# Attention with values as weights in two column halves, logits' products on 128 rows, and layer 0's u splits placed by the scheduler

## The chip, the cores and the metric

One core of one Trainium2 chip runs the whole program in one launch. The metric is the device time of one execution in microseconds (us). TensorE (PE) multiplies, PEld is its weight load, VectorE (DVE) and ScalarE (ACT) do elementwise work, GpSimd (POOL) gathers, SyncE (SP) issues most of the DMAs. Each engine works through its own queue in order.

## What is computed

A decoder step of two layers, d = 1024, for 512 prompt tokens and 8 sample tokens. Layer 0 mixes tokens with a gated delta rule (4 heads, chunks of 64) and a gated linear recurrence (RG-LRU); layer 1 with sliding-window attention (16 query heads, 4 key heads of 64, window 128, a learned sink logit per head). Behind each mixer stands a PEER block: 8 heads pick 16 of 16384 experts, and an expert e adds g_e * v_e * gelu(u_e . x).

```python
x = LN(alpha*x + mixer(x)); x = LN(alpha*x + peer(x))          # each layer
...
logits = (q @ k.T) * 64**-0.5 + bias                           # mixer of layer 1, per head
m = max(logits.max(-1), sink); p = exp(logits - m)             # masked to the window
o = (p / (p.sum(-1) + exp(sink - m))) @ v
...
h = gelu(x @ u_tab.T); y = (gates * h) @ v_tab                 # peer, over the experts picked
```

## The kernel before, in words

A tile scheduler orders each engine's queue: it goes through the program text with a model of each operation's time, and where several instructions are ready, the one that stands earlier in the text goes first. The order on the chip is fixed when the program is built.

Float32 products of projections are made of three float16 products: a number is split into a high half (`split`, first line: ACT copies and rounds, L72) and a low half (second line: DVE takes source times scale less the high half, L79 or L81), and `mm3` (L86 to L88) multiplies high by high, high by low and low by high.

**The u splits.** PEER's dense part multiplies by the table `in_uT` of each layer, block by block. For the first blocks the split halves are made ahead, while a mixer runs, and kept in a DRAM buffer `PW`: `presplit` loads a half block `pst` (128 x 512, 256 KB, issued by SP, L106), splits it to `ppr` (ACT L72, DVE L81) and stores it (SP, L111). `peer` reads `PW` back as `wpr` much later. Layer 0 has 16 blocks or 32 halves, layer 1 has 12 blocks or 24 halves. Before the change `presplit` is a generator. For layer 0 `pstep()` advances it by one half at places chosen in the text of `mixer_ab`: in `new_states`, seven times in the second `inverse`, twice behind each chunk group `rec(n)`, behind each column half of the output projection `mix_out`, with a loop at the end for what is left. `pstep` also ties the half behind the last instruction that DVE and ACT have had in the text (`issue_after`). Each half is one ACT and one DVE instruction of 128 x 512, and `pst` and `ppr` have two buffers each. For layer 1 it is a plain loop behind `mixer_c`, in two pieces of 128 x 256 per half, and the scheduler places it.

**Layer 0's mixer** runs: projections and RG-LRU; `pairs_` (decays `dT`, L1033, and products of the chunks' keys) for chunk groups 0 and 1; `inverse((0, 1))`, with tiles `ia` to `ie` that ACT copies out of PSUM; `zproj` (the z projection, `zth` on ACT, L1169); `pairs_` 2 and 3; `new_states`, which loads the samples' states `S0` (`in_state_gdn`, SP, L1174) and stores the new ones; `inverse((2, 3))`; `rec` (the recurrence over four groups); `mix_out` with `w_out_ab` (residual `mixx`, layer norm L173 to L181, transposes L190, `xh`/`xl`). PEER's queries follow, whose first DVE work is the top-k (L253).

**Layer 1's attention**, `block(n)` for four blocks of 128 queries: for each key-head pair a and head pair q (16 rounds in all), the logits are the sum of a product with the keys' high half `kh` (128 rows, L1444) and one with the low half `kl` (the 64 rows of one half, L1445) for two key heads j and two query heads r; DVE adds the bias and takes the maximum (L1448); ACT takes the exponential and the row sums (L1459); DVE makes the reciprocal of the denominator (L1463); PE transposes the probabilities (L1470), ACT copies them to `pT`; PE multiplies with `pT` as weights (128 columns) and the values `vt` (64 columns) as moving data (L1475, float32, which the trace shows as two records each); DVE multiplies the result by the reciprocal into `ot` (L1477). When a block has its four rounds, PE transposes `ot` in eight pieces (L1484) and `split` makes `mh`, `ml` of it, the moving data of the output projection.

Of the kernel before, what the change touches and what calls it, by code (L numbers as in the profile page):

```python
# [20 lines left out]
PB, PC = 2, 2  # L21
# [44 lines left out]
class Kern:  # L66
# [32 lines left out]
    def presplit(self, pool, layer, n, parts=2):  # L99

        nc, A = self.nc, self.A
        for b in range(n):
            for hf in range(2):
                c = slice(4 * hf, 4 * hf + 4)
                st = pool.tile([P, 4, P], F32, name="pst")
                nc.sync.dma_start(st, A["uT"][layer, b][:, c])  # L106
                o = pool.tile([P, 2, 4, P], F16, name="ppr")
                for q in range(0, 4, 4 // parts):
                    x = slice(q, q + 4 // parts)
                    self.split(o[:, 0, x], o[:, 1, x], st[:, x], SCW)  # L110
                nc.sync.dma_start(self.PW[layer, b, :, :, c], o)  # L111
                yield

    def behind(self, ins):

        ctx = ExitStack()
        for i in ins:
            ctx.enter_context(self.tc.issue_after(i))
        return ctx

    def last_on(self, *engines):

        ins = self.nc.cur_bb.bb.instructions
        return [next(i for i in reversed(ins) if i.engine == e.engine) for e in engines]
# [71 lines left out]
    def mix_out(self, psum, pool, mh, ml, woh, wol, layer, tags, bias=None, bufs=2, step=lambda: None):  # L196
# [12 lines left out]
        for t, t1 in zip(order, order[1:] + (None,)):  # L209
            n = P if t < 4 else NS  # L210
            if t1 is not None:
                load(t1)
            c = slice(t * P, t * P + n)
            x = xs[t][:n]
            if bias is not None:
                nc.vector.tensor_add(x, x, bias[:n])
            if t == 4:

                ps = psum.tile([P, 512], F32, name="pmix", tag=tags[0], bufs=bufs)
                for kb in (4, 5, 6, 7, 0, 1, 2, 3):  # L220
                    for i, (a, b) in enumerate(((mh, woh), (mh, wol), (ml, woh))):
                        for g in range(4):
                            nc.tensor.matmul(ps[32 * g:32 * g + NS, 0:256], a[:, kb, c],
                                             b[kb][:, g * 256:g * 256 + 256], start=kb == 4 and i == 0,
                                             stop=kb == 3 and i == 2)
                s4 = pool.tile([P, 256], F32, name="mixs4")
                s1 = self.wst.tile([P, D], F32, name="wst")[:NS]
                for g in range(4):
                    self.copy(s4[32 * g:32 * g + NS], ps[32 * g:32 * g + NS, 0:256], 1.0 / (SCW * ALPHA))
                    nc.scalar.dma_start(s1[:, g * 256:g * 256 + 256], s4[32 * g:32 * g + NS])  # L230
                nc.vector.tensor_add(x, x, s1)
            for h in range(2 if t < 4 else 0):
# [6 lines left out]
                if t1 is not None:  # L239
                    step()  # L240
# [451 lines left out]
    def mixer_ab(self, ctx):  # L692
# [354 lines left out]
        def inverse(C4, late=False):  # L1047
# [9 lines left out]
            late and pstep()  # L1057
# [11 lines left out]
            late and pstep()  # L1069
# [8 lines left out]
            late and pstep()  # L1078
# [3 lines left out]
            late and pstep()  # L1082
# [3 lines left out]
            for wd in (16, 32):  # L1086
# [3 lines left out]
                late and pstep()  # L1090
# [6 lines left out]
                late and pstep()  # L1097
# [144 lines left out]
        def new_states(ks, vn, egs):  # L1242
# [5 lines left out]
            for q in range(NS):  # L1248
# [5 lines left out]
                if q % 2:  # L1254
                    pstep()
# [19 lines left out]
        inverse((2, 3), True)  # L1275
        ictx.close()
        for n in range(4):
            rec(n)
            pstep()
            pstep()  # L1280
        nc.sync.dma_start(A["o_pgdn"], st)
        with scope("about"):
# [6 lines left out]
            self.mix_out(psum, cur[0], mh, ml, woh, wol, 0, ("g0", "g1", "p", "a"), step=pstep)  # L1289
            for _ in split:  # L1290
                pass
# [41 lines left out]
    def mixer_c(self, ctx):  # L1333
# [38 lines left out]
        kl = w([P, 2, NP], "kl", F16)  # L1372
# [10 lines left out]
        while porder:  # L1383
# [24 lines left out]
            if b in (8, 9):  # L1408
                for j in range(2):
                    o, x = half[j], half[1 - j]  # L1410
                    self.split(kh[o, b - 8, j], kl[o, b - 8], kv[o, b - 8, 0:NP], SQK)
# [17 lines left out]
        def block(n):  # L1429
# [3 lines left out]
            ot = ap_.tile([P, 2, 2, 2, 2, 64], F32, name="ot", bufs=2)  # L1433
            for a in range(2):
                for q in range(2):
# [28 lines left out]
                    po = ps1("o")  # L1464
                    for r in range(2):
                        pt = ps1("t").rearrange("p (j b k) -> p j b k", j=2, b=2)
                        pT = ap_.tile([P, 2, 2, P], F32, name="pT", bufs=4)
# [12 lines left out]
            of = ot.rearrange("p a q r s d -> p (a q r s d)")  # L1480
            for c in range(2):
                pt = ps1("t")
                for k in range(4):
                    T.transpose(pt[:, k * P:k * P + P], of[:, (c * 4 + k) * P:(c * 4 + k + 1) * P], self.ident)  # L1484
                self.split(mh[:, c * 4:c * 4 + 4, tq], ml[:, c * 4:c * 4 + 4, tq],
                           pt.rearrange("p (k t) -> p k t", k=4))
# [74 lines left out]
    def run(self):  # L1561
        nc, tc, A = self.nc, self.tc, self.A
        with ExitStack() as ctx:
# [28 lines left out]
            with ExitStack() as c:  # L1592
                self.mixer_ab(c)
            self.xd = [xd0, xd1]
            self.peer(0)
            with ExitStack() as c:
                pre = self.mixer_c(c)
                for _ in self.presplit(pre, 1, self.NPRE[1]):
                    pass
# [142 lines left out]
```

## Time and profile before

| what | us |
|---|---|
| median of 3 runs | 3039.98 (3039.46 to 3040.66) |
| the profiled execution | 3032.15 |
| its span in the trace | 3030.5 |
| layer 0's mixer | 0 to about 386 |
| layer 0's PEER | to about 1581 |
| layer 1's mixer | to about 1829 |
| layer 1's PEER | to 3030 |

A window's row gives, for each engine, busy time and, in brackets, instructions; PEclk is the granted TensorE clock as a share of full speed. The profiled execution is 7.8 us under the median of the runs.

### The profile page before, as it was taken

The numbers are of one execution on the slowest core, as the hardware profiler recorded it, in microseconds if no ns is written. First come the engines' busy times: TensorE is split into PE (matmuls) and PEld (weight loads), VectorE is DVE, ScalarE is ACT, GpSimd is POOL, SyncE is SP. The second block draws the span as 40 slices with busy tenths as digits, with TensorE's granted clock in tenths as the row PEclk, the third lists the DMA queues.
The fourth block names the chain that finished last, engine by engine and source line by source line (L and its number), as shares of the span: only waits on it lengthen the run. The fifth ranks groups of instructions, "written<-read, shape, count | busy, mean of one in ns | idle before, by whom it ended". The sixth has DMA issues, their size and how long they took to land.

```text
span 3030.5 us, 49817 instructions
## 1 busy us (share of the span) xinstructions
PE 2882.0 (95%) x18342; PEld 1754.9 (58%) x18342; DVE 2557.2 (84%) x5783; ACT 1315.6 (43%) x2131; POOL 838.5 (28%) x661
## 2 busy tenths in 40 slices
PE   8999899899999999999998999989999999999998
PEld 7787586466655555544447568645665555554443
DVE  6755899999878888899986558989987898898998
ACT  4733442356743333333336623335665333343332
POOL 2300101400034555445520000131002445444552
PEclk9998999999999999999999799999999999999999
DMA  4225645965699999999968212586658999999996
GB/s 136 71 81 187 215 126 202 302 225 206 215 375 374 371 359 363 357 352 371 351 243 252 92 63 92 173 303 214 215 202 319 390 363 357 359 360 355 363 356 234
DMA packets 332105, 798.79 MB, mean 264 GB/s; under 512 B 28611, under 2 KB 165259, under 8 KB 328020
## 3 DMA queue, kind: packets, MB, share of 16 engines
q1 hardware_dynamic: 241004, 442.78, 43.2%
q0 software_dynamic: 78336, 285.25, 25.4%
q10 hardware_dynamic: 12520, 67.58, 6.0%
q8 instruction: 143, 2.34, 0.3%
q14 instruction: 102, 0.84, 0.1%
HBM read 700.96 MB, written 93.17 MB: 262 GB/s over the span
## 4 chain that ended last, share of the span: by engine, by line
PE 63%; DVE 15%; DMA 10%; ACT 6%; issue 5%; POOL 1%; SPq 0%; ACTq 0%; DVEq 0%; POOLq 0%
PE yps L623 29%; PE pu L88 6%; PE pu L86 6%; PE pu L87 6%; DMA GD<-stage 3%; ACT stage L72 2%; DMA pst<-in_uT 2%; DVE wl L81 2%; DMA row<-in_u_rows,elist 2%; DVE row L380 1%; PE psg L1009 1%; ACT wh L72 1%; POOL row L373 1%; PE pq L87 1%; PE pq L86 1%
## 5 line engine op out<-in xcount | busy, mean ns | idle before, releaser
L623 PE MATMUL yps<-vv,vw 128*128 128x512 f16 x4536 | 1011.4, 379 | 10.8 <-ACT vv L72 9.0
L623 PEld LDWEIGHTS <-vw 128*128 128x128 f16 x4608 | 450.2, 98 | 542.7 <-issue 16.3
L88 PE MATMUL pu<-xh,wl 128*128 128x384 f16 x1824 | 598.9, 329 | 33.1 <-DVE wl L81 32.7
L373 POOL DMA_INDIRECT row<-in_v_rows,elist x272 | 378.4, 1391 | 886.8 <-ACT stage L72 452.7
L86 PE MATMUL pu<-xh,wh 128*128 128x384 f16 x1824 | 599.4, 329 | 16.1 <-ACT act L349 12.1
L87 PE MATMUL pu<-xl,wh 128*128 128x384 f16 x1824 | 599.6, 329 | 0.0
L373 POOL DMA_INDIRECT row<-in_u_rows,elist x272 | 390.6, 1436 | 673.6 <-DVE best L253 252.2
L72 ACT ACTIVATE wh<-wst 128x1024 f16<-128x1024 f32 x296 | 312.4, 1056 | 554.7 <-PE pu L87 351.2
L81 DVE SCALAR_TENSOR_TENSOR wl<-wst,wh 128x1024 f16<-128x1024 f32 x296 | 361.5, 1222 | 147.2 <-ACT wh L72 136.3
L88 PEld LDWEIGHTS <-wl 128*128 128x128 f16 x2912 | 287.1, 99 | 187.1 <-DVE wl L81 47.0
L86 PEld LDWEIGHTS <-wh 128*128 128x128 f16 x2912 | 289.7, 100 | 160.1 <-ACT wh L72 25.5
L87 PEld LDWEIGHTS <-wh 128*128 128x128 f16 x2912 | 287.2, 99 | 151.8 <-issue 17.8
L72 ACT ACTIVATE vv<-row 128x1024 f16<-128x1024 f32 x252 | 263.2, 1048 | 237.4 <-PE yps L623 183.0
L81 DVE SCALAR_TENSOR_TENSOR vv<-row,vv 128x1024 f16<-128x1024 f32 x252 | 307.7, 1222 | 52.1 <-ACT vv L72 50.6
L561 DVE SCALAR_TENSOR_TENSOR yac<-row,wgt,yac 128x1024 f32<-128x1024 f32 x268 | 343.5, 1282 | 2.8 <-DMA row<-in_v_rows,elist 1.1
L380 DVE CUSTOM_DVE_ANT_0 row<-row,xtok 128x1024 f32<-128x1024 f32 x256 | 308.8, 1220 | 18.9 <-DMA row<-in_u_rows,elist 18.8
L72 ACT ACTIVATE vw<-act 128x384 f16<-128x384 f32 x256 | 129.5, 516 | 349.3 <-PE yps L623 301.1
L72 ACT ACTIVATE stage<-pg 128x512 f32<-128x512 f32 x192 | 183.3, 1107 | 78.3 <-DMA GD<-stage 72.8
L79 DVE TENSOR_TENSOR vw<-act,vw 128x384 f16<-128x384 f32 x256 | 139.5, 553 | 24.1 <-ACT vw L72 23.5
L349 ACT ACTIVATE act<-pu 128x384 f32<-128x384 f32 x256 | 122.4, 479 | 47.3 <-PE pu L88 46.7
L87 PE MATMUL pq<-xl,wh 128*128 128x264 f16 (+1 forms) x480 | 132.2, 275 | 0.9 <-DVE xl L79 0.9
L86 PE MATMUL pq<-xh,wh 128*128 128x264 f16 (+1 forms) x480 | 132.2, 275 | 0.3 <-ACT xh L72 0.3
(500 smaller groups left out, 4018.5 us busy)
## 6 DMA issues: line engine op xcount, KB each, us to landing
row<-in_v_rows SPq DMA_DIRECT2D x256, 512.0 KB
wst<-in_uT SPq DMA_DIRECT2D x228, 512.0 KB
GD<-stage ACTq DMA_DIRECT2D x24, 2048.0 KB
gl<-GD SPq DMA_DIRECT2D x64, 768.0 KB
wst<-in_wq SPq DMA_DIRECT2D x32, 512.0 KB
pst<-in_uT SPq DMA_DIRECT2D x56, 256.0 KB
PW<-ppr SPq DMA_DIRECT2D x56, 256.0 KB
wpr<-PW SPq DMA_DIRECT2D x28, 512.0 KB
```

Of the source, the lines that this page charges most:

```text
L72: self.nc.scalar.activation(out, in_, AF.Copy, scale=scale)
L79: eng.tensor_sub(lo, src, hi)
L81: eng.scalar_tensor_tensor(lo, src, scale, hi, op0=OP.mult, op1=OP.subtract)
L86: mm(out, wh, xh, start=start, stop=False)
L87: mm(out, wh, xl, start=False, stop=False)
L88: mm(out, wl, xh, start=False, stop=stop)
L349: S.activation(t, ps[:, 0:ND], AF.Gelu_apprx_tanh, scale=1.0 / SCW)
L373: G.indirect_dma_start(out=r, out_offset=None, in_=src, in_offset=bass.IndirectOffsetOnAxis(ap=elist[:, k:k + 1], axis=0))
L380: V.tensor_tensor_reduce(u, u, self.xtok[:, 0] if k < P else xrep, 1.0, 0.0, OP.mult, OP.add, hd[:, k:k + 1])
L561: V.scalar_tensor_tensor(dst, vbuf.pop(n), wgt[:, k:k + 1], dst, op0=OP.mult, op1=OP.add)
L623: T.matmul(yps[t][:, o], w[:, a, c], v[:, b, o], start=x == 0 and k == 0, stop=x == P - 1 and k == 2)
L1009: T.matmul(ps[:, h * P:h * P + P], l[:, h], r[:, h], start=True, stop=True)
```

## The change

Layer 0's half blocks are no longer placed by hand: `pstep`, `behind` and `last_on` go, `presplit` becomes a plain loop for both layers, and layer 0's stands behind all of `mixer_ab`, so that the scheduler places it. Its halves are split in two pieces of 128 x 256, with three `pst` buffers; `ppr` keeps two. Layer 1's presplit stays as it was.

In attention, `kl` has zeros in the rows of the other half, and its product runs on 128 rows with the same weights as that of `kh`. The probabilities are normalised before they are transposed (a DVE instruction for each j and r), one `pT` tile takes both r, and the values become the weights: a matmul has 64 columns of weights and 256 columns of moving data, and the two j write the two partition halves of one PSUM tile. This is the transposed output, so `ot`, its multiplication and its transposes go, and `split` reads PSUM once a round.

```diff
-PB, PC = 2, 2
+PB, PC = 4, 2
...
-    def presplit(self, pool, layer, n, parts=2):
+    def presplit(self, pool, layer, n):
...
-                st = pool.tile([P, 4, P], F32, name="pst")
+                st = pool.tile([P, 4, P], F32, name="pst", bufs=PB - 1 if layer == 0 else PC)
                 nc.sync.dma_start(st, A["uT"][layer, b][:, c])
-                o = pool.tile([P, 2, 4, P], F16, name="ppr")
-                for q in range(0, 4, 4 // parts):
-                    x = slice(q, q + 4 // parts)
-                    self.split(o[:, 0, x], o[:, 1, x], st[:, x], SCW)
+                o = pool.tile([P, 2, 4, P], F16, name="ppr", bufs=PB - 2 if layer == 0 else PC)
+                for q in range(0, 4, 2):
+                    self.split(o[:, 0, q:q + 2], o[:, 1, q:q + 2], st[:, q:q + 2], SCW)
                 nc.sync.dma_start(self.PW[layer, b, :, :, c], o)
-                yield
...
-        split = self.presplit(pre, 0, self.NPRE[0], 1)
-
-        def pstep():
-
-            with self.behind(self.last_on(V, S)):
-                next(split, None)
...
-            late and pstep()
...
         for n in range(4):
             rec(n)
-            pstep()
-            pstep()
...
-        kl = w([P, 2, NP], "kl", F16)
+        kl = w([P, 2, 2, NP], "kl", F16)
+        G.memset(kl, 0.0)
...
-                            T.matmul(ps[:, r, k0:256], QS[half[j], j, hp + r, tq], kl[half[j], a, kc],
-                                     start=False, stop=True)
+                            T.matmul(ps[:, r, k0:256], QS[:, j, hp + r, tq], kl[:, j, a, kc], start=False, stop=True)
...
-                    po = ps1("o")
+                    for j in range(2):
+                        for r in range(2):
+                            i = 2 * j + r
+                            V.tensor_scalar(lgt[:, j, r, k0:256], lgt[:, j, r, k0:256], m[:, 2, i:i + 1], None, op0=OP.mult)
+                    pT = ap_.tile([P, 2, 2, 2, P], F32, name="pT", bufs=3)
...
-                        self.copy(pT[:, :, k0 // P:2], pt[:, :, k0 // P:2])
+                        self.copy(pT[:, :, k0 // P:2, r], pt[:, :, k0 // P:2])
+
+                    po = ps1("o")[:, 0:256].rearrange("p (r t) -> p r t", r=2)
+                    for kb in kbs:
                         for j in range(2):
                             g = 2 * a + j
-                            for kb in kbs:
-                                T.matmul(po[:, (2 * j + r) * 64:(2 * j + r) * 64 + 64], pT[:, j, kb],
-                                         vt[:, n - 1 + kb, g * 64:g * 64 + 64], start=kb == kbs[0], stop=kb == 1)
-                    V.tensor_mul(ot[:, a, q].rearrange("p r s d -> p s r d"),
-                                 po[:, 0:256].rearrange("p (s r d) -> p s r d", s=2, r=2),
-                                 m4[:, 2, :, :, None].to_broadcast([P, 2, 2, 64]))
+                            T.matmul(po[half[j]], vt[:, n - 1 + kb, g * 64:g * 64 + 64], pT[:, j, kb],
+                                     start=kb == kbs[0], stop=kb == 1)
+                    self.split(mh[:, hp:hp + 2, tq], ml[:, hp:hp + 2, tq], po)
...
             with ExitStack() as c:
-                self.mixer_ab(c)
+                pre = self.mixer_ab(c)
+                self.presplit(pre, 0, self.NPRE[0])
```

What the scheduler makes of it is seen in the queues. Each row below is one instruction: its line, operation, target and sources, and the target's shape. First SP's queue, from the loads behind layer 0's projections on, before the change:

```order
L1174 DMA S0_2834<-in_state_gdn 128x512
L106 DMA pst_2921<-in_uT 128x512
L106 DMA pst_2945<-in_uT 128x512
L1287 DMA wst_3594<-in_w_out_ab 128x1024
L1174 DMA S0_2840<-in_state_gdn 128x512
L1174 DMA S0_2846<-in_state_gdn 128x512
```

The same place of SP's queue with the change, and the place where the next S0 loads stand, 54 rows on:

```order
L1146 DMA S0_2834<-in_state_gdn 128x512
L106 DMA pst_4031<-in_uT 128x512
L106 DMA pst_4039<-in_uT 128x512
L106 DMA pst_4047<-in_uT 128x512
L110 DMA PW_74<-ppr_4033 256x1x512
L106 DMA pst_4055<-in_uT 128x512
...
L106 DMA pst_4271<-in_uT 128x512
L1146 DMA S0_2840<-in_state_gdn 128x512
L110 DMA PW_74<-ppr_4257 256x1x512
L1146 DMA S0_2846<-in_state_gdn 128x512
```

Twenty-eight of the 32 halves' stores, and the loads between them, now stand ahead of the third and later S0 loads.

ACT's queue at `pairs_` and the first `inverse`, before:

```order
L1033 ACTIVATE dT_2155<-psa_2146,ngc_401 128x128 x4
L1169 ACTIVATE zth_2542<-psp_2486 128x256
L1169 ACTIVATE zth_2545<-psp_2487 128x264
L1033 ACTIVATE dT_2190<-psa_2181,ngc_401 128x128 x4
L1169 ACTIVATE zth_2604<-psp_2548 128x256
L72 ACTIVATE ia_2223<-psg0_2218 128x512
L72 ACTIVATE id_2243<-psg0_2238 128x512
```

The same place with the change:

```order
L1011 ACTIVATE dT_2155<-psa_2146,ngc_401 128x128 x4
L1141 ACTIVATE zth_2542<-psp_2486 128x256
L1141 ACTIVATE zth_2545<-psp_2487 128x264
L72 ACTIVATE ppr_4033<-pst_4031 128x256 x2
L72 ACTIVATE ppr_4041<-pst_4039 128x256 x2
L72 ACTIVATE ppr_4049<-pst_4047 128x256 x2
L72 ACTIVATE ppr_4057<-pst_4055 128x256 x2
L1011 ACTIVATE dT_2190<-psa_2181,ngc_401 128x128 x4
L1141 ACTIVATE zth_2604<-psp_2548 128x256
L72 ACTIVATE ppr_4065<-pst_4063 128x256 x2
L72 ACTIVATE ia_2223<-psg0_2218 128x512
L72 ACTIVATE ppr_4073<-pst_4071 128x256 x2
```

All 64 pieces stand between here and the first instructions of `inverse((2, 3))`; none is left in that inverse, in `rec` or in `mix_out`.

DVE's queue ahead of PEER's first top-k, at the end of layer 0's mixer, before:

```order
L79 TENSOR_TENSOR xl_87<-ptx_4179,xh_86 128x4x128
L81 SCALAR_TENSOR_TENSOR ppr_3983<-pst_3981,ppr_3983 128x512
L81 SCALAR_TENSOR_TENSOR ppr_4015<-pst_4013,ppr_4015 128x512
L81 SCALAR_TENSOR_TENSOR ppr_4188<-pst_4186,ppr_4188 128x512
L81 SCALAR_TENSOR_TENSOR wl_4317<-wst_4314,wh_4316 128x1024
L81 SCALAR_TENSOR_TENSOR ppr_4194<-pst_4192,ppr_4194 128x512
L81 SCALAR_TENSOR_TENSOR wl_4409<-wst_4406,wh_4408 128x1024
L81 SCALAR_TENSOR_TENSOR ppr_4200<-pst_4198,ppr_4200 128x512
L253 MAX st_4246<-scs_4325 128x8 x4
```

The same place with the change:

```order
L164 SCALAR_TENSOR_TENSOR mixx_3809<-mixx_3809,lnmv_4006,lng_3508 128x512 x2
L167 SCALAR_TENSOR_TENSOR xtok_85<-mixx_3809,lnmv_4006,lnb_3509 128x512 x2
L79 TENSOR_TENSOR xl_87<-ptx_4016,xh_86 128x4x128
L79 TENSOR_TENSOR xl_87<-ptx_4023,xh_86 128x4x128
L81 SCALAR_TENSOR_TENSOR wl_4381<-wst_4378,wh_4380 128x1024
L81 SCALAR_TENSOR_TENSOR wl_4473<-wst_4470,wh_4472 128x1024
L237 MAX st_4310<-scs_4389 128x8 x4
```

The five halves that stood between the last xl and the top-k are gone from there.

## Rows read from the trace of the kernel before

**Rows 1.** The page: busy time and share of each engine.

```profile
PE 2882.0 (95%) x18342; PEld 1754.9 (58%) x18342; DVE 2557.2 (84%) x5783; ACT 1315.6 (43%) x2131; POOL 838.5 (28%) x661
```

**Rows 2.** Windows in layer 0's mixer: length, PE, PEld, DVE, ACT, POOL, clock, DMA share, GB/s.

```profile
240.00:250.00 10.00, 10.00 (x91) 9.82 (x90) 3.73 (x12) 4.53 (x8) 0.54 (x1) 1.00 0.20 66
280.00:290.00 10.00, 7.31 (x46) 6.70 (x45) 4.89 (x10) 6.39 (x17) 1.01 (x1) 0.67 0.84 285
290.00:300.00 10.00, 9.43 (x68) 5.50 (x68) 6.95 (x12) 3.64 (x5) 0.00 (x0) 0.66 0.88 322
```

**Rows 3.** Timeline, ACT and DVE, layer 0's end: start, duration, instruction, [idle before].

```profile
362.88 0.63 ACT L72 ACTIVATE ppr<-pst 128x512 f16<-128x512 f32 x1 [7.21 <-DMA pst<-in_uT]
372.65 0.68 DVE L79 TENSOR_TENSOR xl<-ptx,xh 128x512 f16<-128x512 f32 x1
386.27 0.29 DVE L253 MAX8 st<-scs 128x8 f32<-128x128 f32 x1
```

**Rows 4.** Timeline, DVE, the same place in layer 1.

```profile
1822.01 0.69 DVE L79 TENSOR_TENSOR xl<-ptx,xh 128x512 f16<-128x512 f32 x1 [0.40 <-ACT xh L72]
1829.26 0.48 DVE L253 MAX8 st<-scs 128x8 f32<-128x128 f32 x2
```

**Rows 5.** Waits from 250 to 352 us: in total, times, longest.

```profile
ACT ppr L72 <- DMA pst<-in_uT: 18.6, 9, 6.5
```

**Rows 6.** Tile ppr in layer 1: durations (ns, min/median/max), and idle time before it.

```profile
L72 ACT ACTIVATE ppr<-pst x48: 399/403/417, 1588.4 to 1673.7; 128x256 f16<-128x256 f32 x48
  DMA pst<-in_uT: 22.9, 14
```

**Rows 7.** Windows in layer 1's mixer, columns as in rows 2.

```profile
1580.00:1600.00 20.00, 16.99 (x147) 14.09 (x145) 10.04 (x18) 11.88 (x24) 0.00 (x0) 1.00 0.87 279
1640.00:1800.00 160.00, 147.74 (x933) 99.62 (x932) 91.93 (x324) 83.07 (x242) 2.73 (x3) 0.86 0.32 104
```

**Rows 8.** The chain that ended last, near layer 0's end: one load of a half.

```profile
367.36 3.31 DMA pst<-in_uT
```

**Rows 9.** Timeline, SP's DMA issues behind layer 0's projections.

```profile
167.38 2.48 SPq L106 DMA_DIRECT2D pst<-in_uT  x2
...
227.66 15.32 SPq L1174 DMA_DIRECT2D S<-in_state_gdn  x8
```

**Rows 10.** Timeline, PE, attention at full clock (records after x).

```profile
1753.32 0.27 PE L1444 MATMUL psl<-kh,QS 128*128 128x256 f16 x1
1753.53 0.28 PE L1445 MATMUL psl<-kl,QS 64*128 64x256 f16 x1
1753.74 0.28 PE L1444 MATMUL psl<-kh,QS 128*128 128x256 f16 x1
...
1760.21 1.89 PE L1475 MATMUL pso<-vt,pT 128*128 128x64 f32 x16
1761.94 0.60 PE L1470 MATMUL pst<-ident,lgt 128*128 128x128 f32 x4
1762.39 0.60 PE L1484 MATMUL pst<-ident,ot 128*128 128x128 f32 x4
1762.82 0.27 PE L1444 MATMUL psl<-kh,QS 128*128 128x256 f16 x1
```

**Rows 11.** Timeline, PE: 128-row products of 256 columns, and four column groups of samples.

```profile
1640.24 0.27 PE L87 MATMUL psp<-xl,wh 128*128 128x256 f16 x1
1640.35 0.27 PE L88 MATMUL psp<-xh,wl 128*128 128x256 f16 x1
...
297.98 0.28 PE L223 MATMUL pmix<-wol,xh 128*8 128x256 f16 x4
298.09 0.28 PE L223 MATMUL pmix<-woh,xl 128*8 128x256 f16 x4
```

**Rows 12.** Groups of DVE instructions by form: busy, mean ns, idle before.

```profile
L900 DVE TENSOR_SCALAR gg<-gg 128x256 f32<-128x256 f32 x4 | 1.1, 286 | 0.0
L1477 DVE TENSOR_TENSOR ot<-pso,m 128x256 f32<-128x256 f32 x16 | 6.7, 417 | 17.3 <-PE pso L1475 17.0
```

More of the change, by code (lines that the diff above doesn't have):

```diff
@@ L104, in presplit @@
                 c = slice(4 * hf, 4 * hf + 4)
-                st = pool.tile([P, 4, P], F32, name="pst")
+                st = pool.tile([P, 4, P], F32, name="pst", bufs=PB - 1 if layer == 0 else PC)
                 nc.sync.dma_start(st, A["uT"][layer, b][:, c])
-                o = pool.tile([P, 2, 4, P], F16, name="ppr")
-                for q in range(0, 4, 4 // parts):
-                    x = slice(q, q + 4 // parts)
-                    self.split(o[:, 0, x], o[:, 1, x], st[:, x], SCW)
+                o = pool.tile([P, 2, 4, P], F16, name="ppr", bufs=PB - 2 if layer == 0 else PC)
+                for q in range(0, 4, 2):
+                    self.split(o[:, 0, q:q + 2], o[:, 1, q:q + 2], st[:, q:q + 2], SCW)
                 nc.sync.dma_start(self.PW[layer, b, :, :, c], o)
-                yield
[L114 to L124, printed above, removed]
     def ublock(self, layer, b):
@@ L193, in to_xT, with mix_out @@
             self.split(self.xh[:, q * 4:q * 4 + 4, c], self.xl[:, q * 4:q * 4 + 4, c], pt[:, :, :n])
-    def mix_out(self, psum, pool, mh, ml, woh, wol, layer, tags, bias=None, bufs=2, step=lambda: None):
+    def mix_out(self, psum, pool, mh, ml, woh, wol, layer, tags, bias=None, bufs=2):
         nc = self.nc
@@ L238, in mix_out @@
                 nc.vector.scalar_tensor_tensor(x[:, o], ps[:n], 1.0 / (SCW * ALPHA), x[:, o], op0=OP.mult, op1=OP.add)
-                if t1 is not None:
-                    step()
             if t1 is None:
@@ L1045, in pairs_, with inverse @@
             V.tensor_mul(LT[n], pkk, dT)
-        def inverse(C4, late=False):
+        def inverse(C4):
             M1, M1T, M2, M2T, M4, M4T, M8, TM = ({} for _ in range(8))
@@ L1068, in inverse @@
                 V.tensor_add(PT[n], ps, PT[n])
-            late and pstep()
             for n in C4:
@@ L1077, in inverse @@
                 V.tensor_add(PT[n], ps, PT[n])
-            late and pstep()
             for n in C4:
@@ L1081, in inverse @@
                 V.tensor_add(PT[n], ps, PT[n])
-            late and pstep()
             for n in C4:
@@ L1089, in inverse @@
                     B[n] = t4("ia"); V.tensor_mul(B[n], LT[n], hb(om[wd]))
-                late and pstep()
                 for n in C4:
@@ L1096, in inverse @@
                     V.scalar_tensor_tensor(PT[n], ps, -1.0, PT[n], op0=OP.mult, op1=OP.add)
-                late and pstep()
                 for n in C4:
@@ L1274, in mixer_ab @@
         sctx.close()
-        inverse((2, 3), True)
+        inverse((2, 3))
         ictx.close()
@@ L1278, in mixer_ab @@
             rec(n)
-            pstep()
-            pstep()
         nc.sync.dma_start(A["o_pgdn"], st)
@@ L1288, in mixer_ab @@
                 self.split(woh[kb], wol[kb], stg, SCW)
-            self.mix_out(psum, cur[0], mh, ml, woh, wol, 0, ("g0", "g1", "p", "a"), step=pstep)
-            for _ in split:
-                pass
+            self.mix_out(psum, cur[0], mh, ml, woh, wol, 0, ("g0", "g1", "p", "a"))
+        return pre
     def bias_table(self, pool, ps1):
@@ L1410, in mixer_c @@
                     o, x = half[j], half[1 - j]
-                    self.split(kh[o, b - 8, j], kl[o, b - 8], kv[o, b - 8, 0:NP], SQK)
+                    self.split(kh[o, b - 8, j], kl[o, j, b - 8], kv[o, b - 8, 0:NP], SQK)
                     nc.sync.dma_start(kh[x, b - 8, j], kh[o, b - 8, j])
@@ L1432, in block @@
             kbs = range(k0 // P, 2)
-            ot = ap_.tile([P, 2, 2, 2, 2, 64], F32, name="ot", bufs=2)
             for a in range(2):
@@ L1470, in block @@
                                 T.transpose(pt[:, j, kb], lgt[:, j, r, kb * P:kb * P + P], self.ident)
-                        self.copy(pT[:, :, k0 // P:2], pt[:, :, k0 // P:2])
+                        self.copy(pT[:, :, k0 // P:2, r], pt[:, :, k0 // P:2])
+                    po = ps1("o")[:, 0:256].rearrange("p (r t) -> p r t", r=2)
+                    for kb in kbs:
                         for j in range(2):
                             g = 2 * a + j
-                            for kb in kbs:
-                                T.matmul(po[:, (2 * j + r) * 64:(2 * j + r) * 64 + 64], pT[:, j, kb],
-                                         vt[:, n - 1 + kb, g * 64:g * 64 + 64], start=kb == kbs[0], stop=kb == 1)
-                    V.tensor_mul(ot[:, a, q].rearrange("p r s d -> p s r d"),
-                                 po[:, 0:256].rearrange("p (s r d) -> p s r d", s=2, r=2),
-                                 m4[:, 2, :, :, None].to_broadcast([P, 2, 2, 64]))
[L1480 to L1486, printed above, removed]
+                            T.matmul(po[half[j]], vt[:, n - 1 + kb, g * 64:g * 64 + 64], pT[:, j, kb],
+                                     start=kb == kbs[0], stop=kb == 1)
+                    self.split(mh[:, hp:hp + 2, tq], ml[:, hp:hp + 2, tq], po)
         def samples():
@@ L1597, in run @@
                 pre = self.mixer_c(c)
-                for _ in self.presplit(pre, 1, self.NPRE[1]):
-                    pass
+                self.presplit(pre, 1, self.NPRE[1])
             self.peer(1)
```

2 lines of the change are left out of this document (removed).

## Prediction

> **What bounds the kernel now.** I read the page first: TensorE is busy 95% of the span, VectorE 84%, ScalarE 43% [rows 1]. The reader should see that time is won where PE becomes shorter, or where PE stands idle or at its lower clock, and that work on ACT or DVE costs only through waits. The change touches two stretches, so I read the windows of each.
>
> In layer 0's mixer the first part is PE-bound: at 240 to 250 us PE is busy all 10 us, with ACT at 4.53, DVE at 3.73 and the DMAs at 0.20 [rows 2], and the stretch from 170 on looks like it. From 250 on it is not. At 280 to 290 PE is busy 7.31, at 290 to 300 9.43, and the granted clock is 0.67 and 0.66, between the levels of 1.2 and 2.4 GHz, behind a stretch in which PE had idled; the DMAs are at 0.84 and 0.88 [rows 2]. There the waits name the u splits: ACT stood 18.6 us in nine waits for `pst` [rows 5], and one of 7.21 us follows at 362.88 [rows 3]. ACT's queue is in order, so the copies of the recurrence and of the layer norm's transposes stand behind each of those.
>
> In attention, the window of 160 us has PE busy 147.74 (92%) at a mean clock of 0.86, DVE 91.93, ACT 83.07 [rows 7]: PE bounds it, with some room on the other two.
>
> **The u splits, step by step.** Removed: 32 ACT and 32 DVE instructions of 128x512 spread over 250 to 394 us. Added: 64 and 64 of 128x256, which cost about 0.40 us each on ACT [rows 6], 26 us in all and about as much on DVE. The order shows them from about 167 us to the start of the second inverse, some 75 to 80 us, with no room lacking on average: ACT at 4.5 and DVE at 3.7 of 10 have it.
>
> Gain one, the tail. The last `xl` ends at 373.33 and top-k starts at 386.27, 12.9 us later [rows 3]; in layer 1, where no u split stands there, the same way takes 1829.26 - 1822.70 = 6.6 us [rows 4]. All the halves are gone from the tail, so I take 12.9 - 6.6 = 6.3 us. It can't be fully hidden: nothing else is ahead of that top-k in DVE's queue but two `wl` splits, which layer 1 has too.
>
> Gain two, the middle. In 280 to 300 PE idles 2.69 + 0.57 us, and the clock loses 0.33 x 10 + 0.34 x 10 = 6.7 us; with 7.2 us at 362 the sum is about 17. A part of it is the chain of small products itself, with one step waiting for the copy of the last. I take a third, 6 us; the ends are 0 and 17.
>
> Loss, the front. ACT will meet `ppr` between `dT` and `zth`, before their loads have come. One load took 3.31 us [rows 8]; with the issue, the split and a store behind it, three `pst` and two `ppr` buffers let one half through in some 2 to 2.5 us. SP issued its first two at 167.38 [rows 9], so 28 halves end around 167 + 5 + 28 x 2.4 = 239, and behind them stand the S0 loads that SP issued from 227.66 to 243 [rows 9]. So they are up to 12 us late, and the second half of `new_states` with them. What scheduler-placed halves cost PE is seen in layer 1: in 1580 to 1600, where they run, PE is busy 16.99 of 20 us [rows 7], 15% less than at 240 to 250, with 22.9 us of ACT's waits for `pst` [rows 6]. If all 15% came from them, 80 us here would lose 12 us. But other transfers hold the DMAs there at 0.87 and here they are nearly idle, so I take 8 us; the ends are 0 (PE's filler work hides it, as the 0.20 DMA share speaks for) and 30 (below). The Trainium skill ("TensorE: Matmul & The Clock Gate", engine queue depths) says that ScalarE and VectorE are strict in-order queues while TensorE may only pull weight loads ahead, which speaks against this part: by that rule each wait for `pst` is passed on to all of ACT. The trace agrees so far as the 7.21 us wait ended with a burst of ACT work behind it, and no run here shows what it would cost in the front.
>
> Sum of the first part: -6.3 - 6 + 8 = -4 us, between -23 and +17.
>
> **Attention, step by step.** All at full clock, per round with two key blocks (12 of the 16).
>
> The logits: one product on 128 rows and one on 64 are 0.21 us each, eight of them 1.70 us [rows 10]. Products of the same 256 columns on 128 rows follow each other every 0.11 us [rows 11]. With 128 rows for both, 8 x 0.11 = 0.88 us. I take this as sure, since shape and type are the same.
>
> The transposes of the probabilities stay: 0.45 us for four [rows 10], 0.90 a round.
>
> The values: 1761.94 - 1760.21 = 1.73 us a round for 16 records [rows 10]. After: four products of 256 float32 columns, two records each. A record of 128 float32 columns takes 0.11 us (the transposes), so one of 256 takes 0.225, and the round 4 x 2 x 0.225 = 1.80 us alone, or 0.90 where the two column halves run at the same time. That column groups do so is seen in the samples' projection: four groups' products go in one record of 0.11 us pitch [rows 11]. No row shows it for float32 weights or for 64 columns, so the ends are 0.90 and 1.80; I take 0.90, as row 297.98 is the nearest, and 0.2 for going in and out of the mode. The Trainium skill ("TensorEngine Tiling (Array Packing)", Tiling Modes, Key Properties) says that tiles work in parallel, and that a change of mode drains the array. The trace bears out the second at 64 rows: the pitch of 0.21 us there against 0.11. By the rule alone the sum stays as it is, since the change takes away eight changes of mode a round and adds two.
>
> The transposes of `ot`: 0.43 us for four [rows 10], two a round, 0.22 us, gone.
>
> Round before: 1.70 + 0.90 + 1.73 + 0.22 = 4.55. After: 0.88 + 0.90 + 1.10 = 2.88, or 3.78 without overlap. Saved: 1.67 (0.77). Twelve rounds save 20 (9), the four of the first block, with one key block, about half, 3 (2). So 23 us of PE time, or 11.
>
> What of it is on the path: PE is 92% busy in the stretch, and its lower clock makes each saved record longer. Against that, DVE gets four multiplications of 0.286 us a round and loses one of 0.417 [rows 12], +0.73, 12 us over 16 rounds on an engine that is 57% busy [rows 7], and the round's chain grows by about 1.1 us, since normalising now stands ahead of the transposes. The splits of the output read PSUM in pieces half as long, about even. The output projection's products fill PE while a round waits, but some of a shorter PE then shows as idle. I take about half: 12 us. The ends are 0 (DVE and the chain set the pace) and 26 (all of 23, part at the lower clock).
>
> **Sum.** -4 - 12 = -16 us against the profiled execution's 3032.15, so 3016; the runs' median lies 7.8 us above it, and I carry that along: 3039.98 - 16 = 3024 us. About 0.2% (6 us) is what a measurement can tell from no change.
>
> **The rivals.**
>
> *The front paces layer 0 (slower).* If a half takes the 3.7 us that it takes in layer 1 (24 halves, 48 pieces, whose first and last start at 1588.4 and 1673.7 [rows 6]), 28 halves need 104 us, not 67, and S0 loads come at about 275, some 40 us late. PE's own work there runs dry behind 250, as the 7.31 of 280 to 290 shows [rows 2], so some 30 us are lost, of which the gains return 12; with attention at -12 the sum is +6, and with attention at the low end +15: 3046 to 3055. It decides from about 3.2 us a half. For it: SP's strict alternation, one load behind one store. Against: the DMAs are at 0.20 at 240 us and the layer 1 stretch at 0.87, and three buffers instead of two. Chance 0.16.
>
> *Attention gives nothing (about the same).* The chain through DVE and ACT grows and PE idles instead; with the first part at 0 to -4 it ends at 3035 to 3040. For it: DVE already waited 17 us for a round's result [rows 12], a chain with no slack, and `pT` loses a buffer. Against: PE at 92%. Chance 0.15.
>
> *Both give all (much faster).* Column halves overlap, the clock rises in 280 to 300, and the front costs nothing: -12 - 20 = -32, 3008. Chance 0.14.
>
> The forecast, both parts about as worked out, 3015 to 3034: chance 0.55. Faster than 3034 takes the forecast, the last case and a little of the second: 0.70; within 0.2%: 0.15; slower: 0.15. The range leaves out the lowest part of the third and the upper part of the first: 3006 to 3046.
>
> **What would show it.** Right: no `ppr` behind about 250 us; the way from the last `xl` to top-k at 6 to 7 us; PE above 9.5 in the front; L1412's records 0.11 us apart; values' pairs of both halves starting together; PE time of attention 20 us shorter. Wrong: ACT waiting for `pst` in front of `dT` and `ia` with PE idle at 170 to 240; S0 loads after 250 us; values' records 0.22 apart; DVE's new multiplications at the head of PE's waits in attention.

## The result and the profile after

| | before | with the change |
|---|---|---|
| median of 4 runs, us | 3040.32 (3039.46 to 3041.34) | 3010.43 (3006.40 to 3011.95) |
| ratio | | 0.990, 95% interval 0.9882 to 0.9917 |
| profiled execution, us | 3032.15 | 3010.68 |
| layer 0's first top-k (L253, now L237), us from the span's start | 386.27 | 393.38 |
| first projection product of layer 1 | 1582.62 | 1591.71 |
| layer 1's first top-k | 1829.26 | 1807.50 |

The change saves about 30 us (1.0%), in the two profiled executions 21.5: the profiled execution before lies 8 us under its median, the one after at it. The marks say where. Layer 0's mixer became longer by 7.1 us. The way from the first projection product of layer 1 to its first top-k, called layer 1's mixer below, went from 246.64 to 215.79 us, 30.9 less. Layer 0's PEER between them took 2.0 us more. So one part of the forecast had the wrong sign and the other was too small by more than half.

Two windows of the front and the back of layer 0's mixer, first before, in the columns of [rows 2]:

```profile
170.00:260.00 90.00, 88.39 (x766) 82.50 (x764) 44.03 (x87) 33.80 (x70) 1.08 (x2) 1.00 0.18 57
260.00:390.00 130.00, 116.10 (x762) 76.19 (x763) 97.78 (x195) 55.10 (x117) 9.43 (x9) 0.91 0.71 234
```

The same windows after:

```profile
170.00:260.00 90.00, 74.60 (x584) 68.30 (x583) 53.17 (x122) 44.33 (x115) 0.66 (x1) 0.91 0.72 222
260.00:390.00 130.00, 122.66 (x860) 84.79 (x859) 87.44 (x171) 45.74 (x100) 10.05 (x10) 0.97 0.37 125
```

The front lost 13.8 us of PE's busy time and, as an estimate, 0.09 x 90 = 8 us of clock; the back got 6.6 us of busy time and 0.06 x 130 = 8 us of clock. ACT is far from full in the front (44.33 of 90), so it is not work but waits that cost there. The timeline of ACT after, at `pairs_` 0 and 1:

```profile
166.28 1.14 ACT L1011 ACTIVATE dT<-psa,ngc 128x128 f32<-128x128 f32 x4 [3.54 <-PE psa L1008]
177.31 1.35 ACT L72 ACTIVATE ppr<-pst 128x256 f16<-128x256 f32 x4 [9.34 <-DMA pst<-in_uT]
181.09 0.72 ACT L72 ACTIVATE ppr<-pst 128x256 f16<-128x256 f32 x2 [2.43 <-DMA PW<-ppr]
184.75 0.72 ACT L72 ACTIVATE ppr<-pst 128x256 f16<-128x256 f32 x2 [2.94 <-DMA PW<-ppr]
185.38 1.12 ACT L1011 ACTIVATE dT<-psa,ngc 128x128 f32<-128x128 f32 x4
```

The second group of `dT` stands behind four halves in ACT's queue and comes 19 us after the first. SP's timeline, same stretch:

```profile
162.55 0.63 SPq L1278 DMA_DIRECT2D bd<-bt  x1
163.22 2.99 SPq L1286 DMA_DIRECT2D sbd<-sbt  x1
166.26 2.57 SPq L1146 DMA_DIRECT2D S<-in_state_gdn  x2
168.92 3.14 SPq L106 DMA_DIRECT2D pst<-in_uT  x3
178.55 0.53 SPq L110 DMA_DIRECT2D PW<-ppr  x1
...
244.91 0.40 SPq L1146 DMA_DIRECT2D S<-in_state_gdn  x1
```

The three first loads of `pst` are issued behind `bd`, the store of layer 1's bias table (3 MB), and the first lands at 177.2. The third S0 load comes at 244.91 and not at 227.66 [rows 9]. The waits from 160 to 260 us after show what else holds ACT (in total, times, longest):

```profile
ACT ppr L72 <- DMA PW<-ppr: 25.1, 19, 2.9
ACT ppr L72 <- DMA pst<-in_uT: 9.3, 1, 9.3
```

The chain that ended last says that this is what paces the front. From 160 to 260 us after, stores of `PW` are 31.8% of it and loads of `pst` 8.3%, where before PE's own products led it (L1009, 32.0%). The first load and one of the stores (start, duration):

```profile
168.92 8.29 DMA pst<-in_uT
195.33 4.37 DMA PW<-ppr
```

DVE at the end of layer 0's mixer after, the counterpart of [rows 3]:

```profile
384.35 0.69 DVE L79 TENSOR_TENSOR xl<-ptx,xh 128x512 f16<-128x512 f32 x1 [0.40 <-ACT xh L72]
393.38 0.87 DVE L237 MAX8 st<-scs 128x8 f32<-128x128 f32 x4
```

From 385.04 to 393.38 are 8.3 us, where before there were 12.9.

In layer 1, first the whole mixer before, then after:

```profile
1582.62:1829.26 246.64, 222.85 (x1531) 158.47 (x1530) 144.09 (x432) 128.28 (x347) 4.56 (x5) 0.90 0.44 141
```

```profile
1591.71:1807.50 215.79, 186.71 (x1387) 128.84 (x1386) 152.67 (x487) 128.08 (x355) 4.56 (x5) 0.94 0.50 161
```

PE's busy time fell by 36.1 us and its idle time rose from 23.8 to 29.1. As an estimate, the clock lost 0.10 x 246.64 = 24.7 us before and 0.06 x 215.79 = 12.9 after, at a mean between the levels of 1.2 and 2.4 GHz. DVE got 8.6 us more. PE's timeline of a round after, the counterpart of [rows 10]:

```profile
1719.96 1.08 PE L1446 MATMUL pso<-pT,vt 128*64 128x256 f32 x8
1720.97 0.66 PE L1439 MATMUL pst<-ident,lgt 128*128 128x128 f32 x4
...
1722.54 0.27 PE L1411 MATMUL psl<-kh,QS 128*128 128x256 f16 x1
1722.65 0.27 PE L1412 MATMUL psl<-kl,QS 128*128 128x256 f16 x1
1722.76 0.27 PE L1411 MATMUL psl<-kh,QS 128*128 128x256 f16 x1
```

Logits 0.11 us apart, as forecast; a round's values take 1720.97 - 1719.96 = 1.01 us, where 1.10 was forecast. The eight records of the values start in pairs. The same group as the timeline counts it up to 1720.2, 1720.4 and 1720.65 us:

```profile
1719.96 0.44 PE L1446 MATMUL pso<-pT,vt 128*64 128x256 f32 x2
1719.96 0.65 PE L1446 MATMUL pso<-pT,vt 128*64 128x256 f32 x4
1719.96 0.87 PE L1446 MATMUL pso<-pT,vt 128*64 128x256 f32 x6
```

Each further 0.22 us brings two records. Where the weights have 128 columns, in the samples' attention, the same time brings one (counted up to 1689.5 and 1689.7 us):

```profile
1689.31 0.38 PE L1492 MATMUL pso<-vc,pz 128*128 128x256 f32 x1
1689.31 0.60 PE L1492 MATMUL pso<-vc,pz 128*128 128x256 f32 x2
```

### The profile page after: what moved, and what is told of

Read it like the earlier page. It is cut to its first block, busy times and chain, and to the rows that moved or that the text cites. A ratio compares the mean times of both kernels' runs of the same rounds, so it can differ in the third digit from the quotient of the medians.

```text
span 3008.9 us, 49598 instructions
## 1 busy us (share of the span) xinstructions
PE 2845.8 (95%) x18198; PEld 1726.9 (57%) x18198; DVE 2569.4 (85%) x5871; ACT 1319.3 (44%) x2171; POOL 856.1 (28%) x662
## 4 chain that ended last, share of the span: by engine, by line
PE 66%; DVE 13%; DMA 10%; ACT 6%; issue 4%; POOL 1%; SPq 0%; ACTq 0%; DVEq 0%; POOLq 0%
PE yps L607 30%; PE pu L88 7%; PE pu L86 7%; PE pu L87 7%; DMA row<-in_u_rows,elist 2%; ACT stage L72 2%; PE pq L87 2%; DMA GD<-stage 2%; PE pq L86 2%; PE pq L88 2%; DVE wl L81 2%; DMA pst<-in_uT 2%; DVE row L364 1%; DMA PW<-ppr 1%; DMA gl<-GD 1%
## 5 line engine op out<-in xcount | busy, mean ns | idle before, releaser
L357 POOL DMA_INDIRECT row<-in_v_rows,elist x272 | 395.4, 1454 | 862.9 <-issue 251.0
L88 PE MATMUL pq<-xh,wl 128*128 128x264 f16 (+1 forms) x480 | 132.9, 277 | 0.0
```

The costliest lines, as they stand in the source:

```text
L88: mm(out, wl, xh, start=False, stop=stop)
L357: G.indirect_dma_start(out=r, out_offset=None, in_=src, in_offset=bass.IndirectOffsetOnAxis(ap=elist[:, k:k + 1], axis=0))
```

## The experiments

The first four take the parts of the change singly.

**attn_only**: the kernel before with the new `mixer_c`.

```diff
         for n in range(4):
             rec(n)
+            pstep()
+            pstep()
...
```

(That is, seen from the change, the placement by hand comes back.)

> The kernel before with the attention edits alone; layer 0's u splits stay placed by hand. If the profiles are right that attention gave about 31 us (layer 1's mixer 246.6 to 215.8 us) and the scheduler's placement of the u splits cost about 7 to 9 us (first top-k 386.3 to 393.4 us), this is the fastest so far: about 31 us under before, 3009, and its first top-k is at 386. Rival, by the forecast's own sum (attention -12, u splits -4): about 12 us under before.

Measured: 3012.58 us, ratio 0.9926 (0.9904 to 0.9947), 22 us less by the ratio, where 31 was expected. First top-k at 388.75, layer 1's mixer 215.68 us. The attention edits carry most of the gain in time and all of it in the marks, and the forecast's -12 for them is out. The runs of before spread over 3023.57 to 3047.04 here, 26 of them, so single times tell little under 10 us; the marks in the trace tell more.

**splits_only**: the change with the old `mixer_c`.

> The change's placement of layer 0's u splits alone; attention as before. If it costs in the front what the profile after shows, 7 to 9 us slower than before, ACT waiting about 9 us for its first pst at 170 to 180 us, first top-k at 393. Rival, the forecast: 4 us faster.

Measured: 3042.86 us, ratio 1.0026 (1.0010 to 1.0042): slower by 8 us (3 to 13). First top-k at 390.94, layer 1's mixer, with the old attention, 244.40 us; ACT's wait for the first `pst` is there again. The sign is against the forecast.

**kl_only**: before with the low half on 128 rows.

```diff
-        kl = w([P, 2, NP], "kl", F16)
+        kl = w([P, 2, 2, NP], "kl", F16)
+        G.memset(kl, 0.0)
...
-                            T.matmul(ps[:, r, k0:256], QS[half[j], j, hp + r, tq], kl[half[j], a, kc],
-                                     start=False, stop=True)
+                            T.matmul(ps[:, r, k0:256], QS[:, j, hp + r, tq], kl[:, j, a, kc], start=False, stop=True)
```

> The kernel before, with only the low half of the keys on 128 rows (zeros in the other half). Pitch of the logits' products 0.21 to 0.11 us at full clock: 0.85 us for each of 12 rounds and half that for 4, so 12 us of PE time. If PE's work sets the time there, 10 to 13 us faster; if the chain through DVE and ACT does, under 4 us.

Measured: 3025.69 us, ratio 0.9973 (0.9956 to 0.9990). Layer 1's mixer 232.99 us, 13.65 less. PE's timeline, where L1445 and L1446 are the two products now:

```profile
1747.16 0.27 PE L1445 MATMUL psl<-kh,QS 128*128 128x256 f16 x1
1747.27 0.27 PE L1446 MATMUL psl<-kl,QS 128*128 128x256 f16 x1
1747.38 0.27 PE L1445 MATMUL psl<-kh,QS 128*128 128x256 f16 x1
```

The product does twice the rows' work in half the time, and all of the 12 us saved on PE arrive in the stage; in total time the ratio gives 8 us (3 to 13).

**values_only**: the attention edits with `kl` as before.

> The attention edits without that of the keys' low half: values as weights in two column halves, probabilities normalised first. PE saves 1.73 + 0.22 - 1.01 = 0.94 us a round at full clock, about 13 us in all, while each round's chain on DVE grows. If PE sets the time, 10 to 14 us faster and, with kl_only, the sum of both is about that of both edits together; if the longer chain counts, under 6 us and the sum falls short.

Measured: 3025.34 us, ratio 0.9958 (0.9944 to 0.9973). Layer 1's mixer 228.17 us, 18.5 less. With kl_only's 13.65 that makes 32.1, and both edits together give 30.9: they add up. No cost of the longer chain on DVE shows.

The next ones ask what the placement of the u splits costs.

**changed_again**: the changed kernel, beside the next three.

> The changed kernel as it is, beside the next three on one chip. The parts alone were -0.74% and +0.26%: if they add up, it is 0.5% (15 us) under before; if it is again 1% (30 us) under, the two parts help each other, or the first measurement of it had a favourable set of runs.

Measured: 3008.99 us, ratio 0.9908 (0.9883 to 0.9932); first top-k at 396.09, ACT waits 9.35 us for the first `pst`. So the first measurement stands. In time the parts alone (-0.74% and +0.26%) do not add up to it; hand_again below, with -0.95% for the first of them, closes part of the gap, and the rest stays open.

**bd_early**: the bias table is made earlier in the text.

```diff
+            self.bias_table(cpool, ps1)
             for h in range(4):
                 lru(h)
...
-        self.bias_table(cpool, ps1)
         cctx.close()
```

> The changed kernel with the bias table (bd, a 3 MB store) made between RG-LRU's two loops instead of behind them. If the 9.3 us in which ACT waited for the first pst come from that store, which is issued 6 us ahead of it, the wait falls below 4 us, the second dT group comes some 10 us earlier than 185 us, PE is busy over 9 in 170 to 190 (4.88 and 7.47 before), and top-k comes 5 us earlier, 386 to 388. Rival: the wait only moves to the next halves, since ppr waits for its stores anyway (25 us in 19 waits); then top-k stays at 391 to 393.

Measured: 2996.49 us, ratio 0.987 (0.9843 to 0.9896), the fastest kernel here that leaves nothing out: 1.3% under before and 12.5 us under changed_again, each of its five runs under each of the other's six. First top-k at 378.62. The store is issued at 82.00 instead of 162.55. ACT:

```profile
161.80 1.14 ACT L1011 ACTIVATE dT<-psa,ngc 128x128 f32<-128x128 f32 x4 [3.40 <-PE psa L1008]
164.32 1.42 ACT L72 ACTIVATE ppr<-pst 128x256 f16<-128x256 f32 x4 [1.38 <-DMA pst<-in_uT]
168.09 0.72 ACT L72 ACTIVATE ppr<-pst 128x256 f16<-128x256 f32 x2 [1.58 <-DMA PW<-ppr]
171.16 1.14 ACT L1011 ACTIVATE dT<-psa,ngc 128x128 f32<-128x128 f32 x4
```

The wait of 9.3 us is 1.4, the second `dT` comes 9.4 us after the first and at 171.16 instead of 185.38, and PE is busy 10.00 us at 170 to 180. The gain in top-k is 15 to 17 us, that of the second `dT` 14.2. Of those 14.2, 4.5 are the first `dT`'s (161.80 for 166.28), since the table's own work has gone from there too, and 9.7 the waits. That the earlier `dT` makes all of the gain in top-k is not shown: bd_early_ppr3 below has its second `dT` at 171.88 and its first top-k at 386.26, 7.6 us later than here. At 180 to 190 PE is busy 8.24, less than the 9 expected, and ACT's waits for `PW`'s stores stay (27.7 us).

**hand_early**: attn_only with the same edit.

> The attention edits with u splits placed by hand, and the bias table made between RG-LRU's two loops as in bd_early. With the table behind them, the first dT group came at 166 us, with it ahead at 162; so some 4 us of bd_early's gain (top-k at 378.6 instead of 393 to 396) should be seen here too, and 10 to 13 us not, since no split stands in front of the second dT group in this order: top-k at 384 to 385, time 4 us under attn_only. Rival: the early table helps any placement alike, and top-k comes 14 us earlier, at 375.

Measured: 3015.18 us, ratio 0.9924 (0.9904 to 0.9944), no gain over attn_only, and its first top-k at 393.31, which neither theory expected. The first `dT` comes at 159.94, 6.5 us earlier than in attn_only, but the windows show it lost again: at a lower clock in the front (0.85 for 1.00), and with PE less busy behind 260 (107.80 for 116.31). First attn_only, then hand_early:

```profile
170.00:260.00 90.00, 88.67 (x771) 82.91 (x769) 42.86 (x86) 33.23 (x68) 1.08 (x2) 1.00 0.19 58
260.00:390.00 130.00, 116.31 (x755) 75.95 (x756) 96.67 (x182) 54.29 (x116) 9.44 (x9) 0.89 0.72 233
```

```profile
170.00:260.00 90.00, 89.69 (x676) 85.65 (x675) 37.75 (x76) 31.29 (x64) 1.08 (x2) 0.85 0.10 30
260.00:390.00 130.00, 107.80 (x718) 69.45 (x716) 96.10 (x177) 53.38 (x113) 8.76 (x9) 0.93 0.70 230
```

So the early table gave nothing in time with the order by hand, and 12.5 us with the scheduler's, where splits stand ahead of `dT`. Why the clock fell here is open, so the marks of this run do not say what the table is worth alone.

**no_splits**: no half is split in layer 0's mixer; the 32 stores write zeros, so PEER's products with those 16 blocks are left out in effect.

```diff
-                self.presplit(pre, 0, self.NPRE[0])
+                z = pre.tile([P, 2, 4, P], F16, name="ppr", bufs=1)
+                self.nc.gpsimd.memset(z, 0.0)
+                for b in range(self.NPRE[0]):
+                    for hf in range(2):
+                        self.nc.sync.dma_start(self.PW[0, b, :, :, 4 * hf:4 * hf + 4], z)
```

> The changed kernel without layer 0's u splits: 32 stores of zeros stand in for them (no loads, no ACT or DVE work), so the experts of those 16 blocks get wrong products. It gives the floor of both placements. If the splits by the scheduler cost what the front's idle PE shows, about 16 us of idle time and 7 us of clock, top-k comes at 375 or earlier; if other waits take their place, at 383 to 388.

Measured: 2993.15 us, ratio 0.986 (0.983 to 0.9891); first top-k at 372.55. So of layer 0's mixer the splits cost 21 to 24 us in the change and its repeat, 14 to 17 in the order by hand, 6 in bd_early and 14 in bd_early_ppr3. In time the kernel is 16 us under changed_again. The front:

```profile
170.00:260.00 90.00, 88.89 (x765) 83.83 (x762) 41.92 (x84) 31.91 (x66) 2.03 (x3) 0.98 0.43 140
```

With the stores there (DMA share 0.43), but no `ppr` in ACT's queue, PE is as busy as before the change. The loads are gone here too, but in bd_early, with both, PE is busy 10.00 at 170 to 180 us at a DMA share of 0.72. It is the waits in ACT's and DVE's queues that empty PE, not the traffic.

**ppr3** and **bd_early_ppr3**: two `pst` and three `ppr` buffers, in the change and in bd_early.

```diff
-                st = pool.tile([P, 4, P], F32, name="pst", bufs=PB - 1 if layer == 0 else PC)
+                st = pool.tile([P, 4, P], F32, name="pst", bufs=PB - 2 if layer == 0 else PC)
...
-                o = pool.tile([P, 2, 4, P], F16, name="ppr", bufs=PB - 2 if layer == 0 else PC)
+                o = pool.tile([P, 2, 4, P], F16, name="ppr", bufs=PB - 1 if layer == 0 else PC)
```

> The changed kernel with two pst and three ppr buffers for layer 0 instead of three and two. If the 25 us of ACT's waits for PW's stores are what costs, they fall under 8 us and the time by 3 to 5 us. If five buffers in all give the same pace whichever way they are split, as many waits for pst come in their place and the time is within 2 us of the changed kernel's.

> bd_early with two pst and three ppr buffers. There, ACT still waits 27.7 us in 22 waits for PW's stores. In ppr3 the waits only went over to pst (29.7 us) and the time stayed; if that holds here too, it is within 3 us of bd_early, 2996. If a store's wait costs more than a load's, 4 us less.

Measured: 3009.03 us (0.9905, 0.9874 to 0.9936) and 3001.98 us (0.9875, 0.9854 to 0.9895), the same as changed_again and as bd_early within their intervals. In ppr3 ACT waits 29.7 us in 16 waits for `pst` where the change had 25.1 in 19 for `PW` and its repeat 19.3 in 15. Which side has the third buffer makes no difference in time that these runs show. bd_early_ppr3 was expected within 3 us of 2996, and its median is 5.5 above it; its four runs go from 2992.75 to 3006.33, and the profiled one, with the first top-k at 386.26, is the slowest of them. More than five buffers were not run.

**hand_again**: attn_only once more.

> attn_only once more, beside hand_early on one chip. Its ratio to the kernel before was 0.9926, that of the change 0.9900 and 0.9908 in two other sets: if the u splits' placement costs what splits_only showed (+0.26%), it stays under the change's ratio; if the three are one within their spread, it is at about 0.991.

Measured: 3008.64 us, ratio 0.9905 (0.9889 to 0.9921); first top-k at 389.56. So in total time the change (0.9900, 0.9908) and attn_only (0.9926, 0.9905) can't be told apart; splits_only, 0.26% slower than before, is the only set that shows a cost of the placement by time. In the marks they can: first top-k at 390.9, 392.3, 393.4 and 396.1 in the four kernels with the scheduler's order (splits_only, ppr3, the change and its repeat), and at 386.3 to 389.6 in the six with the order by hand and the late table, one profiled execution each.

**halves_apart**: attn_only, the values' products in another order.

```diff
-                    for kb in kbs:
-                        for j in range(2):
+                    for j in range(2):
+                        for kb in kbs:
                             g = 2 * a + j
```

> The attention edits (u splits by hand) with the values' products in the order both key blocks of one column half, then both of the other, so that neighbours use the same half three times in four. If the two halves run at the same time only when neighbours differ, a round's values take about 1.5 us instead of 1.01, and layer 1's mixer 5 to 8 us longer than attn_only's 215.7. If the array doesn't overlap them, or orders them itself, nothing changes.

Measured: 3010.98 us, ratio 0.9915 (0.9899 to 0.9931). A round's eight records take 1.09 us, first start to last end, as against 1.08 in attn_only. Layer 1's mixer takes 219.72 us, 4.0 more than attn_only's, but hand_again, the same kernel as attn_only, has 218.76. So the order of the halves makes no difference in time, and the records start in pairs here too (the group up to 1705.2 and 1705.4 us, and whole):

```profile
1704.96 0.44 PE L1479 MATMUL pso<-pT,vt 128*64 128x256 f32 x2
1704.96 0.66 PE L1479 MATMUL pso<-pT,vt 128*64 128x256 f32 x4
1704.96 1.09 PE L1479 MATMUL pso<-pT,vt 128*64 128x256 f32 x8
```

In the trace's starts, the two of a pair are 7 ns apart in the change and in attn_only, where the records of the two halves stand two places apart in the text, and 12 to 14 ns here, where they stand four places apart, but again 6 to 8 ns here in the first block's rounds, where they stand two places apart. That fits pairs of one record from each half. Which half a record writes the trace does not say.

## Why the prediction was right and where it was not

The total lies in the range, and faster by over 0.2% was right. Its steps did not all hold, and that the sum came out in the range is in part luck: in the marks attention gave 19 us more than forecast (30.9 for 12), and the u splits cost 7 where 4 were to be gained, an error of 11 the other way. A further 8 us of the 30 are the distance of the profiled execution before from its median, which the forecast carried along and which was not there after. At 3010 the result is under the 3015 to 3034 that had the chance of 0.55, and near the 3008 of the case that both parts give all; but that case had the front cost nothing, and the front cost 22.

- **The logits** (1.70 to 0.88 us a round): right, 0.11 us a record, and kl_only shows it on the path.
- **The values** (1.73 to 1.10): right, 1.01, and by the reason given as far as the rows show. The records start in four pairs some 0.22 us apart, and a record with 128 columns of weights takes the same 0.22 alone (0.225 in the sum). So 64 columns of weights bring two records in the time of one, 4 x 0.22 = 0.88, and 0.13 is left where the forecast put 0.2 without a row. What it did not foresee is that the two halves need not be neighbours in the text: halves_apart is as fast.
- **"I take about half: 12 us" of attention's 23**: this step failed. All of it arrived, and more: 30.9 = 36.1 us less busy time of PE, less 5.3 us more idle time. Of the 36.1, 11.7 are the clock's, which lost 24.7 us before and 12.9 after; the rest, 24.4, is the 23 of the sum. The window's 92% was the thing to go by, with the lower clock on top; the DVE work and the longer chain, for which half was taken off, cost nothing that values_only shows. That the output projection's products hid them is likely and not shown. The size holds beyond the one pair: the ten kernels with the new attention have a layer 1's mixer of 213.7 to 219.7 us, the two with the old one 246.64 and 244.40.
- **The tail** (6.3): 12.9 to 8.3, 4.6. **The middle** (6 of 17): with the tail, the back gained 6.6 + 8 = 14 us, where 12.3 was forecast. Together they held, with less from the tail.
- **"Loss, the front: I take 8 us"**: mis-sized. It was 13.8 us of PE's time and 8 of clock, 22, inside the ends of 0 and 30. The pace was right: from the first landing at 177.2 to the third S0 load at 244.91, 28 halves took 2.4 us each, as forecast, so the first rival, which needs 3.2, did not come about. What the sum missed is the store of the bias table ahead of the first load: the sum had the first load land some 5 us behind 167, and it landed at 177.2; the S0 load came 17 us late, not 12. The store could be read in the trace of the kernel before, where SP issues it 6.4 us ahead of its first `pst`. The other part of the error is the price of the pace itself: the forecast took it low because the DMAs were nearly idle there (0.18 in the window before), and with the change the halves hold them at 0.72, and ACT waits 25.1 us for their stores. Moving the table, in bd_early, was worth 12.5 us in time; how much of that is the wait alone stays open.
- So the u splits' part came out at about +5 in the marks (+7 in the profiled pair, +8 in splits_only's time), not -4. Between the change and attn_only, total time does not show it.
- Three figures of the prediction do not follow from its own terms, and none decided: by its ends the first part goes up to -6.3 + 30 = +24, not +17; the first rival with attention at its low end of 0 gives +18, not +15; and S0 loads at 275 would be 47 us late, not 40.
- Of the signs named beforehand, these came: logits 0.11 us apart, values in pairs, over 20 us less PE time in attention. These did not: 6 to 7 us to top-k (8.3) and a front above 9.5 of 10 (74.60 of 90). And of the signs of being wrong one came: ACT waiting for `pst` in front of `dT`, with PE at 4.88 of 10 at 170 to 180 us.
- Single runs of the kernel before spread over 25 us, far more than the 0.2% that the forecast took as the limit of a measurement; the intervals of the ratios here are 0.15 to 0.3% either way.

The Trainium skill ("TensorE: Matmul & The Clock Gate", engine queue depths) has ScalarE as a strict in-order queue; the trace agrees, with the second `dT` at 185.38 behind the 9.34 us wait and at 171.16 where that wait was 1.38 (bd_early).

## What to carry to other kernels

Work that a scheduler may place freely is not free: on an in-order queue each of its waits for a transfer is passed to all that stands behind, so look at what the DMA queues still have to move when its first load is issued. Where PE was 92% busy, PE work saved came back at its full price and more, so take it so in such a stretch, and look at the clock beside it. Give a matmul the shape of its neighbours: a product on 128 rows, half of them zeros, took half the time of one on 64 rows between 128-row ones. Where the weights have 64 columns and there are two sets of them, two products into the two halves of the output took the time of one.

## What was not expected of the hardware

- Float32 records of 256 columns with 64 columns of weights went two at a time, a pair every 0.22 us, as often as one record with 128 columns of weights; and they did so also where the records of one half stood together in the text (halves_apart).
- A load of 256 KB, issued 6.4 us behind a 3 MB store, with a small store and two more loads of 256 KB between, took 8.29 us from its issue at 168.92, where one near layer 0's end took 3.31 [rows 8]. With the store over 75 us ahead (bd_early), ACT started on the first half 4.8 us after its load's issue.
- A front in which PE was fuller (89.69 of 90 us, hand_early) ran at a clock of 0.85, and one with 88.67 (attn_only) at 1.00. What set the clock there is open.
